# Two more ring buffers, four result tiles and back-to-back sums in a fused decoder layer

## The chip, the cores and the metric

The kernel runs on one core of a Trainium2 chip. The metric is the device time of one execution in microseconds (us), lower is better; a time is the median of several runs. On the core, TensorE (PE in the profile) multiplies matrices, and its weight loads (PEld) overlap with that; VectorE (DVE) and ScalarE (ACT) do elementwise work; GpSimd (POOL) and SyncE (SP) do little else here than issue DMAs between the chip's memory (HBM) and the on-chip SBUF. Results of the matmuls land in PSUM banks, which DVE and ACT empty. Each engine works through its own list in order; semaphores hold an instruction back until what it needs is there.

## The reference

One layer of a decoder in float32, for 1024 prompt tokens (and 16 learned meta tokens ahead of them) and 32 sample tokens: a gated short convolution and a multi-scale retention side by side, a projection, and a dense SwiGLU FFN, each behind an RMS norm. Cut to what matters:

```python
def _rmsnorm(x, g):
    y = x * lax.rsqrt(jnp.mean(x * x, axis=-1, keepdims=True) + EPS)
    return y * g

def _layer(x, ...):
    z = _rmsnorm(x, norm1_g) @ w_in                     # 1024 -> 3584
    conv_out = b_gate * conv(c_gate * h)                # 512 wide
    ret_out  = silu(g) * norm(retention(q, k, v))       # 512 wide
    x = x + concat([conv_out, ret_out]) @ w_out
    xn = _rmsnorm(x, norm2_g)
    return x + (silu(xn @ w_gate) * (xn @ w_up)) @ w_down   # 1024 -> 2816 -> 1024

y_prompt, y_sample = _rmsnorm(layer output, final_norm_g)   # and the new conv and retention states
```

## The kernel before

Activations lie transposed: 128 features on the partitions, tokens along the free axis. Every fp32 matrix product is made of three matmuls of a rounded part ("hi", tiles ending in `h` or called `whi`) and a rest ("lo", ending in `l` or called `wlo`): hi·hi, hi·lo, lo·hi. ACT makes each hi by a copy, DVE each lo by a subtraction.

The program runs in this order. First come the input projections with the two mixers, then `w_out`, which also builds the operands of the FFN. The **up phase** is a loop over 22 pairs of feature tiles (`f`, L861 on). Each takes one 2x2 step of Strassen's method in Winograd's form (`strassen`, L750): seven products instead of eight. The products go into three banks: y (`by`, four products y1 to y4), z (`bz`) and w (`bw`). Behind each product, `on` (L884) reads the bank; y3 for example is added to `up` by L894, and y4, which goes on in the same bank, cannot start before that add has read it.

What the up phase computes does not fit into SBUF. `spill` (L798) writes the operands of nine pairs of `f` to HBM (`hd`): seven operands each (b11, t3, t1, t2, t4, b21, b22), of which four are differences (`td`, L795: tiles dt3, dt1, dt2, dt4). For each operand `to_hd` (L788) takes two ring buffers, fills them (`hh` by ACT at L790, `hl` by DVE at L791), and GpSimd writes them out (L792, L793). One operand is put out at each step of the following `f`, through the generator `pending`. The last four `f` are put out plainly (`spill_plain`, tensor `hp`).

All of these are buffers of one ring: the pool `rows`, tag "u", with 60 buffers (L126, `ut`). During the up phase 56 of them hold the operands of the FFN, so that four pass the spilled pairs. A tile that takes a buffer waits until everything that used the buffer's last tile is done, the DMA that wrote it out included.

The **down phase** reads the operands back (`pull_block`, L840, `pull`, L833, tiles `hb..` and `ht..`) in four blocks into the same ring, and multiplies them by `w_down` with the same Strassen step, two output tiles (`m`, `m+1`) at a time. Its `on` adds each product to the residual `x1` (L958). SyncE issues the pulls and the loads of `w_down` (L153) in one list. A pull is issued when its buffer is free; the first block's pulls are spread over the last `f`, four at each step. The sums of weight quarters that Strassen's method needs (s1 to s4) are made by `total` at L754 on DVE.

The end is the plain part (`pd`, L999): for each of four groups of tokens (two sets of tokens, two halves) it runs through eight tiles `m`, adds to `x1` (L1004), sums the squares, and `finish` (L972) makes the final norm. `rms_compact` (L204) sums over the partitions by matmuls with a column of ones, once for each of the two partial sums (`ss3` and the last square `sq3`), and DVE combines them (L220, L222). After the root (L198 to L202) and the broadcast (`n3b`), each result tile `yt` takes two multiplies on DVE (L984), and SyncE writes it to `o_y` (L985), 256 KB. There are two `yt` buffers for four result tiles a group. The finish of the first three groups runs beside the matmuls of the next group, one step for each `m` (`tail`); that of the last has nothing beside it.

The order of the instructions on every engine is settled when the program is built, by a scheduler that knows the pools and their sizes. So a change of a pool's size moves instructions that the source leaves where they were.

Of the kernel before, what the change touches and what calls it, by code (L numbers as in the profile page):

```python
# [10 lines left out]
F32 = mybir.dt.float32  # L11
F32R = mybir.dt.float32r
AF = mybir.ActivationFunctionType
# [3 lines left out]
P = 128  # L17
# [4 lines left out]
NSAMP = NS * TS  # L22
NMETA = 16
# [6 lines left out]
HD = 64  # L30
# [10 lines left out]
SG = 544  # L41
# [5 lines left out]
HT = 528  # L47
# [71 lines left out]
def _body(nc, tc, t, offs, ncols):  # L119
    PSUM = bass.MemoryType.PSUM  # L120
    V, S, G, T, D = nc.vector, nc.scalar, nc.gpsimd, nc.tensor, nc.sync
    HW = SG // 2
    with contextlib.ExitStack() as ctx:
        cst = ctx.enter_context(tc.tile_pool(name="cst", bufs=1))
        wts = ctx.enter_context(tc.tile_pool(name="wts", bufs=4))
        rows = ctx.enter_context(tc.tile_pool(name="rows", bufs=60))  # L126
        acc = ctx.enter_context(tc.tile_pool(name="acc", bufs=3, space=PSUM))
        aux = ctx.enter_context(tc.tile_pool(name="aux", bufs=2, space=PSUM))
        dram = ctx.enter_context(tc.tile_pool(name="dram", bufs=1, space=bass.MemoryType.DRAM))
# [1 line left out]
        def ut(name, dt=F32):  # L131
            return rows.tile([P, SW], dt, tag="u", name=name)
# [71 lines left out]
        def rms_compact(sets, name):  # L204
            blocks = [(i, o, min(P, w - o)) for i, (_, w) in enumerate(sets) for o in range(0, w, P)]
            tot = len(blocks)
            ps = aux.tile([P, 512], F32, tag="aux", name=name + "p")
            a = cst.tile([P, 16], F32, tag="rms", name=name + "a", bufs=6)
            V.memset(a, 1.0)
            for q in range(len(sets[0][0])):  # L210
                for i, (c, o, n) in enumerate(blocks):
                    T.matmul(ps[:n, q * tot + i:q * tot + i + 1], sets[c][0][q][:, o:o + n], ones[:, 0:1],
                             start=True, stop=True)
                i = 0
                while i < tot:
                    j, n = i, blocks[i][2]
                    while j < tot and blocks[j][2] == n:
                        j += 1
                    if q == 0:
                        V.tensor_scalar(a[:n, i:j], ps[:n, i:j], 1.0 / DM, EPS, ALU.mult, ALU.add)  # L220
                    else:
                        V.scalar_tensor_tensor(a[:n, i:j], ps[:n, q * tot + i:q * tot + j], 1.0 / DM, a[:n, i:j],  # L222
                                               ALU.mult, ALU.add)
# [22 lines left out]
        with contextlib.ExitStack() as mid_ctx:  # L246
# [46 lines left out]
            for k in range(KT):  # L293
# [82 lines left out]
            kT = []  # L376

            vt = [mid.tile([P, 4, 512], F32, name=f"v{s}") for s in range(SETS)]
            vs = mid.tile([NSAMP, 512], F32, name="vs")
            vm = mid.tile([NMETA, 512], F32, name="vm")  # L380
            def v_rows(vT, j, s):
                pt = aux.tile([P, 4, P], F32, tag="aux", name="pvt")
                for b in range(4):
                    T.transpose(pt[:, b, :], vT[:, b * P:(b + 1) * P], ident)
                S.activation(vt[s][:, :, j * P:(j + 1) * P], pt, AF.Copy)
                if s == 0:
                    pe = aux.tile([P, 2, P], F32, tag="aux", name="pve")
                    for i, (ex, o, ne) in enumerate(((vs, 512, NSAMP), (vm, 544, NMETA))):
                        T.transpose(pe[:ne, i], vT[:, o:o + ne], ident)
                        S.activation(ex[:, j * P:(j + 1) * P], pe[:ne, i], AF.Copy)  # L390

            held = None
            for j in range(4):
# [50 lines left out]
            def meta_and_samples():  # L444
# [7 lines left out]
                ps = aux.tile([P, NPAIR, P], F32, tag="aux", name="ps0")  # L452
                kf = kmd.rearrange("p h d -> p (h d)")
                for j in range(4):
                    T.matmul(ps[:, j, :], kf[:NMETA, j * P:(j + 1) * P], vm[:, j * P:(j + 1) * P],
                             start=True, stop=True)
                for hh in range(2):
                    sl = slice(hh * HD, (hh + 1) * HD)
# [20 lines left out]
                pms = []  # L479
# [29 lines left out]
                for h in range(H):  # L509
                    for n2 in range(4):  # L510
                        T.matmul(po[:NSAMP, h, :], qx[h % 2][:, n2, h // 2, :], sst[h][:, n2 * HD:(n2 + 1) * HD],
                                 start=(n2 == 0), stop=False)
                    T.matmul(po[:NSAMP, h, :], pms[h % 2][:NSAMP, h // 2, :], vs[:, h * HD:(h + 1) * HD],
                             start=False, stop=True)
                    if h == 3:
                        yield
                yield
                d = group_norm(po, NSAMP, "sgam", "sgam2")
                for h2 in range(4):
                    pn = aux.tile([P, 2, 256], F32, tag="aux", name="psn")  # L520
                    for a in range(2):
                        h = 2 * h2 + a
                        kv = ut("kv")
                        for p in range(2):
                            G.tensor_copy(kv[:NSAMP, p * HD:(p + 1) * HD], kd[p][:NSAMP, h, :])
                        for n2 in range(4):
                            V.tensor_scalar(kv[:NSAMP, P + n2 * HD:P + (n2 + 1) * HD], vs[:, h * HD:(h + 1) * HD],
                                            tb("nsel")[:NSAMP, n2:n2 + 1], None, ALU.mult)
# [175 lines left out]

        for s in range(SETS):
            n = ntok[s]
            ss2 = late.tile([P, SG], F32, tag="rr", name="ss2", bufs=2)
            half = None
            for m in range(KT):
                x = gg("x1")  # L710
# [261 lines left out]
        def finish(s, g, ss3, q):  # L972
            n = ntok[s]
            oc = slice(OOFF[s] + g * n, OOFF[s] + (g + 1) * n)
            r, blocks = rms_compact([([ss3, q], n)], "n3")
            yield
            pb = aux.tile([P, 512], F32, tag="aux", name="n3b")
            for i, (_, o, w) in enumerate(blocks):
                T.matmul(pb[:, o:o + w], r[:w, i:i + 1].broadcast_to([w, P]), ident[:w, :w], start=True, stop=True)
            for m in range(0, KT, 2):  # L980
                yt = fin.tile([P, SG], F32, tag="yt", name="yt", bufs=2)
                y2 = yt[:, :2 * n].rearrange("p (g n) -> p g n", g=2)
                for i in range(2):
                    V.tensor_tensor(y2[:, i, :], x1[m + i][g][:, SO[s]:SO[s] + n], pb[:, :n], ALU.mult)  # L984
                D.dma_start(yo[:, m:m + 2, oc], y2)  # L985
                yield
# [91 lines left out]
```

## Time and profile before

| | |
|---|---|
| median of 3 runs | 1218.04 us (1217.74 to 1219.55) |
| the profiled execution's own time | 1217.98 us |
| its span, first to last instruction | 1216.2 us |
| mean granted TensorE clock | 0.993 |
| PE busy | 1190.3 us, 98% of the span |
| DVE, ACT, POOL busy | 844.7, 487.2, 121.3 us |
| moved by DMA | 162.91 MB, 134 GB/s on average |

The span is that of the one execution the profiler recorded; its own time has 1.8 us around the span. In the rows below, a timeline row has the start and the duration in us, engine, line, operation, and output<-inputs; "[idle before <-releaser]" is how long the engine stood still before it and what it waited for last. A row of the waits has the total, the number of times, and the longest. A row of the windows has the window, its length, each engine's busy time with the number of instructions, the granted clock (PEclk), the busy share of the DMA engines, and the GB/s moved.

### The profile page before, as it was taken

To read this page: it belongs to the slowest core of one execution; us is meant where nothing else is said; L and a number is where in the kernel's file an instruction comes from. 1 tells how busy PE (TensorE), PEld (TensorE's weight loads), DVE (VectorE), ACT (ScalarE), POOL (GpSimd) and SP (SyncE) were. 2 spreads that over 40 slices of the span, in tenths; PEclk is the share of its full clock that TensorE was granted. 3 is DMA by queue.
4 is the path that set the end of the run, shared out by engine and by line. 5 is a ranking of instruction groups with operands and counts; after the bars stand their busy time and mean duration, and the time that the engine had idled before them with its cause. 6 is when DMAs were issued, how large, how long until landed. Compare 5 with 4: busy or idle time off the path is not lost.

```text
span 1216.2 us, 22825 instructions
## 1 busy us (share of the span) xinstructions
PE 1190.3 (98%) x8903; PEld 1135.4 (93%) x8903; DVE 844.7 (69%) x1591; ACT 487.2 (40%) x932; POOL 121.3 (10%) x251
## 2 busy tenths in 40 slices
PE   8999999999999999999999999999999899999996
PEld 6998988999989998899999999999999899999996
DVE  5454467676554577877877787787876588887655
ACT  8246531121233456544443544444344222222353
POOL 0100112000100012102211221121121000000000
PEclk9999999999999999999999999999999999999998
DMA  6231211000111356425433543454254998864213
GB/s 232 80 98 35 79 36 61 27 27 27 48 46 44 99 176 195 148 71 186 151 111 137 186 151 104 145 179 144 90 191 129 388 349 271 307 212 162 93 39 106
DMA packets 82059, 162.91 MB, mean 134 GB/s; under 512 B 10702, under 2 KB 23776, under 8 KB 81952
## 3 DMA queue, kind: packets, MB, share of 16 engines
q1 hardware_dynamic: 67568, 114.57, 28.7%
q0 software_dynamic: 14384, 46.88, 11.1%
q8 instruction: 70, 1.15, 0.4%
q14 instruction: 37, 0.30, 0.1%
HBM read 113.15 MB, written 48.26 MB: 133 GB/s over the span
## 4 chain that ended last, share of the span: by engine, by line
PE 64%; issue 22%; DMA 5%; POOL 4%; DVE 3%; ACT 2%; SPq 0%; POOLq 0%; DVEq 0%; ACTq 0%
PE dy L766 8%; PE po L186 8%; PE by L766 4%; PE dz L766 4%; PE pc L186 4%; PE pd L999 4%; PE pg L186 4%; PE pq L186 4%; PE ph L186 4%; PE pv L186 4%; PE pb L186 3%; PE pk L186 3%; PE dw L766 2%; PE bz L766 2%; POOL hd L793 2%
## 5 line engine op out<-in xcount | busy, mean ns | idle before, releaser
L158 ACT ACTIVATE whi<-wraw 128x512 fp32r<-128x512 f32 (+2 forms) x198 | 115.7, 584 | 291.0 <-issue 49.8
L160 DVE TENSOR_TENSOR wlo<-wraw,whi 128x512 fp32r<-128x512 f32 (+2 forms) x198 | 124.4, 629 | 54.9 <-ACT whi L158 54.8
L158 ACT ACTIVATE whi<-s 128x512 fp32r<-128x512 f32 (+2 forms) x152 | 83.8, 552 | 162.4 <-PE by L766 47.7
L766 PE MATMUL by<-b,whi 128*128 128x256 f32 (+1 forms) x704 | 129.9, 285 | 1.4 <-DVE up L894 1.4
L766 PE MATMUL bz<-t,whi 128*128 128x256 f32 (+1 forms) x704 | 130.5, 284 | 0.3 <-DVE t L691 0.3
L766 PE MATMUL by<-t,whi 128*128 128x256 f32 (+1 forms) x704 | 130.3, 284 | 0.0
L160 DVE TENSOR_TENSOR wlo<-s,whi 128x512 fp32r<-128x512 f32 (+2 forms) x152 | 89.3, 587 | 31.6 <-ACT whi L158 31.5
L766 PEld LDWEIGHTS by<-b,whi 128*128 128x128 f32 x704 | 109.2, 188 | 2.2 <-DVE up L894 2.0
L766 PEld LDWEIGHTS bz<-t,whi 128*128 128x128 f32 x704 | 109.3, 188 | 0.5 <-DVE t L691 0.5
L766 PEld LDWEIGHTS by<-t,whi 128*128 128x128 f32 x704 | 108.9, 188 | 0.1
L766 PE MATMUL bz<-t,wlo 128*128 128x256 f32 (+1 forms) x352 | 100.1, 284 | 0.0
L766 PE MATMUL by<-b,wlo 128*128 128x256 f32 (+1 forms) x352 | 100.0, 284 | 0.0
L766 PE MATMUL by<-t,wlo 128*128 128x256 f32 (+1 forms) x352 | 100.0, 284 | 0.0
L766 PEld LDWEIGHTS by<-b,wlo 128*128 128x128 f32 x352 | 66.3, 188 | 0.0
L766 PEld LDWEIGHTS by<-t,wlo 128*128 128x128 f32 x352 | 66.3, 188 | 0.0
L766 PEld LDWEIGHTS bz<-t,wlo 128*128 128x128 f32 x352 | 66.3, 188 | 0.0
L766 PE MATMUL bw<-b,whi 128*128 128x272 f32 (+1 forms) x352 | 65.1, 284 | 0.0
L958 DVE TENSOR_TENSOR x<-x,dy 128x528 f32<-128x528 f32 x64 | 45.0, 704 | 26.0 <-PE dy L766 25.4
L792 POOL DMA_DIRECT2D hd<-hh x63 | 34.0, 540 | 271.7 <-ACT hh L790 271.3
L766 PE MATMUL dz<-ht,whi 128*128 128x256 f32 (+1 forms) x288 | 54.9, 287 | 3.9 <-ACT whi L158 3.9
L766 PE MATMUL dy<-hb,whi 128*128 128x256 f32 (+1 forms) x288 | 53.3, 284 | 2.8 <-ACT whi L158 2.8
L766 PE MATMUL dy<-ht,whi 128*128 128x256 f32 (+1 forms) x288 | 54.5, 286 | 0.1
(303 smaller groups left out, 3094.8 us busy)
## 6 DMA issues: line engine op xcount, KB each, us to landing
ht<-hd SPq DMA_DIRECT2D x72, 264.0 KB, 5.4
hd<-hh POOLq DMA_DIRECT2D x63, 264.0 KB, 3.0
hd<-hl POOLq DMA_DIRECT2D x63, 264.0 KB, 3.2
hb<-hd SPq DMA_DIRECT2D x54, 264.0 KB, 5.4
wraw<-w_in SPq DMA_DIRECT2D x54, 256.0 KB, 2.6
wraw<-w_gate SPq DMA_DIRECT2D x44, 256.0 KB, 2.6
wraw<-w_up SPq DMA_DIRECT2D x44, 256.0 KB, 2.7
wraw<-w_out SPq DMA_DIRECT2D x32, 256.0 KB, 2.8
```

The source lines that it names most:

```text
L158: S.activation(hi[:, :n], raw[:, :n], AF.Copy)
L160: V.tensor_tensor(lo[:, :n], raw[:, :n], hi.bitcast(F32)[:, :n], ALU.subtract)
L186: T.matmul(ps[:, g, :n], wt[:, sl], xk[part][:, g * n:(g + 1) * n], start=(first and i == 0), stop=(last and i == 2))
L766: T.matmul(out, wt[:, sl], rhs(s, k, key, part), start=(first and k == 0 and i == 0), stop=(k == kt - 1 and i == 2), skip_group_check=not ...
L792: G.dma_start(dst[0], hi.bitcast(F32)[:, :HT])
L793: G.dma_start(dst[1], lo.bitcast(F32)[:, :HT])
L958: V.tensor_tensor(x, x, ps, ALU.subtract if i else ALU.add)
L999: T.matmul(ps[:, 0, :n], wt[:, sl], hs[k][g][part][:, SO[s]:SO[s] + n], start=(k == 0 and i == 0), stop=(k == NPL - 1 and i == 2))
```

## The change

Five edits:

1. The ring `rows` has 62 buffers instead of 60.
2. `vs` and `vm`, two small tiles of the value projection that had room of their own in the pool `mid`, are now ring tiles (a part of a 128-row buffer is used).
3. The spill's differences (`td`) share the buffers of the tag "rr" with `ss2`, instead of having three of their own; "rr" has three buffers instead of two. By then `ss2` is done with.
4. The result tile `yt` has four buffers instead of two.
5. In `rms_compact` the ones-matmuls of all partial sums stand ahead of all DVE instructions that combine them. For a norm with one partial sum nothing changes; the final norm, `n3`, has two.

```diff
-        rows = ctx.enter_context(tc.tile_pool(name="rows", bufs=60))
+        rows = ctx.enter_context(tc.tile_pool(name="rows", bufs=62))
...
-            for q in range(len(sets[0][0])):
+            nq = len(sets[0][0])
+            for q in range(nq):
                 for i, (c, o, n) in enumerate(blocks):
                     T.matmul(ps[:n, q * tot + i:q * tot + i + 1], sets[c][0][q][:, o:o + n], ones[:, 0:1],
                              start=True, stop=True)
+            for q in range(nq):
                 i = 0
                 while i < tot:
...
-            vs = mid.tile([NSAMP, 512], F32, name="vs")
-            vm = mid.tile([NMETA, 512], F32, name="vm")
+            vs = ut("vs")
+            vm = ut("vm")
...
-            ss2 = late.tile([P, SG], F32, tag="rr", name="ss2", bufs=2)
+            ss2 = late.tile([P, SG], F32, tag="rr", name="ss2", bufs=3)
...
         def td(name):
-            return late.tile([P, HT], F32, tag="td", name=name, bufs=3)
+            return late.tile([P, SG], F32, tag="rr", name=name, bufs=3)[:, :HT]
...
-                yt = fin.tile([P, SG], F32, tag="yt", name="yt", bufs=2)
+                yt = fin.tile([P, SG], F32, tag="yt", name="yt", bufs=4)
```

The number of instructions of the layer stays; three places show how their order and their waits move. Lines from L211 on are two higher in the changed kernel.

DVE's list in the up phase, `f` = 16, between the spill's difference dt4 and the add of y3 (`up_9254<-by`). `hl_9442` belongs to dt4, `hl_9479` to b21, `hl_9514` to b22. Before:

```order
L160 TENSOR_TENSOR wlo_9451<-wraw_9247,whi_9449 128x512 [waits PE_49,Activation_49]
L791 TENSOR_TENSOR hl_9405<-dt2_9402,hh_9404 128x528 [waits DMASW3_49,DMASW0_49,DMASW4_49,DVE_49,Activation_49]
L160 TENSOR_TENSOR wlo_9486<-s4_9447,whi_9484 128x512 [waits PE_49,Activation_49]
L754 TENSOR_TENSOR s4_9692<-s2_9603,wraw_9532 128x512 [waits DMAHW0_49,DVE_49]
L791 TENSOR_TENSOR hl_9442<-dt4_9439,hh_9441 128x528 [waits DMASW5_49,Activation_49]
L791 TENSOR_TENSOR hl_9479<-up_9020,hh_9478 128x528 [waits DMASW7_49,Activation_49]
L892 TENSOR_TENSOR gt_9251<-bw_9257,gt_9251 128x528 [waits PE_49]
L160 TENSOR_TENSOR wlo_9543<-wraw_9526,whi_9541 128x512 [waits Activation_49]
L908 TENSOR_TENSOR gt_9251<-gt_9251,rstd2_3941 128x528 [waits DVE_49]
L791 TENSOR_TENSOR hl_9514<-up_9021,hh_9513 128x528 [waits DMASW2_49,DMASW6_49,DMASW1_49,Activation_49]
L894 TENSOR_TENSOR up_9254<-by_9255,up_9254 128x528 [waits PE_49]
```

The same place after the change:

```order
L160 TENSOR_TENSOR wlo_9451<-wraw_9247,whi_9449 128x512 [waits PE_49,Activation_49]
L793 TENSOR_TENSOR hl_9405<-dt2_9402,hh_9404 128x528 [waits DMASW1_49,Activation_49]
L793 TENSOR_TENSOR hl_9442<-dt4_9439,hh_9441 128x528 [waits DMASW3_49,DMASW4_49,DMASW2_49,DMASW6_49,DMASW0_49,Activation_49]
L160 TENSOR_TENSOR wlo_9486<-s4_9447,whi_9484 128x512 [waits PE_49,Activation_49]
L756 TENSOR_TENSOR s4_9692<-s2_9603,wraw_9532 128x512 [waits DMAHW0_49,DVE_49]
L793 TENSOR_TENSOR hl_9479<-up_9020,hh_9478 128x528 [waits DMASW5_49,Activation_49]
L793 TENSOR_TENSOR hl_9514<-up_9021,hh_9513 128x528 [waits DMASW7_49,Activation_49]
L894 TENSOR_TENSOR gt_9251<-bw_9257,gt_9251 128x528 [waits PE_49]
L160 TENSOR_TENSOR wlo_9543<-wraw_9526,whi_9541 128x512 [waits Activation_49]
L910 TENSOR_TENSOR gt_9251<-gt_9251,rstd2_3941 128x528 [waits DVE_49]
L896 TENSOR_TENSOR up_9254<-by_9255,up_9254 128x528 [waits PE_49]
```

`hl` of b22 no longer stands directly ahead of the add of y3 but four places earlier, ahead of the add of the w bank; `hl` of dt4 stands two places earlier, ahead of the split of s4. On ACT `hh` of dt4 likewise moves ahead of the split of s4 and the copy of y2. On GpSimd the writes of `hh` and `hl` alternate now. The waits on DMAs (DMASW) name other writes.

SP's list at the change from up to down phase: the last pulls of block 0 (`hb22`), loads of `w_down` (`wraw_10863` is the fourth for the first pair of output tiles, `wraw_11009` to `wraw_11013` the first three for the second pair), and the pulls of block 1 (`hb11`, `ht3`). Before:

```order
L835 DMA hb22_10832<-hd_3939 128x528
L153 DMA wraw_10863<-w_down 128x256
L835 DMA hb11_10885<-hd_3939 128x528
L835 DMA hb11_10906<-hd_3939 128x528
L835 DMA hb11_10929<-hd_3939 128x528
L835 DMA hb11_10948<-hd_3939 128x528
L835 DMA ht3_10967<-hd_3939 128x528
L835 DMA ht3_10988<-hd_3939 128x528
L835 DMA ht3_11007<-hd_3939 128x528
L153 DMA wraw_11009<-w_down 128x256
L153 DMA wraw_11011<-w_down 128x256
L153 DMA wraw_11013<-w_down 128x256
```

After:

```order
L837 DMA hb22_10832<-hd_3939 128x528
L153 DMA wraw_11009<-w_down 128x256
L837 DMA hb11_10885<-hd_3939 128x528
L837 DMA hb11_10906<-hd_3939 128x528
L837 DMA hb11_10929<-hd_3939 128x528
L837 DMA hb11_10948<-hd_3939 128x528
L837 DMA ht3_10967<-hd_3939 128x528
L837 DMA ht3_10988<-hd_3939 128x528
L837 DMA ht3_11007<-hd_3939 128x528
L153 DMA wraw_11011<-w_down 128x256
L153 DMA wraw_11013<-w_down 128x256
```

`wraw_11009` has moved ahead of seven pulls, while `wraw_11011` and `wraw_11013` stay at the same number of DMAs from the list's start; `wraw_10863` has moved 24 places forward, to just behind the fourth pull of block 0.

DVE's list at the very end, the last group's norm and its result tiles (`n3p` are the sums in PSUM, `n3a` the mean square, `n3r` the inverse root). Before:

```order
L220 TENSOR_SCALAR n3a_14217<-n3p_14216 128x2 [waits PE_49]
L222 SCALAR_TENSOR_TENSOR n3a_14217<-n3p_14216,n3a_14217 128x2 [waits DVE_49,PE_49]
...
L984 TENSOR_TENSOR yt_14235<-x1_10546,n3b_14232 128x256 [waits DMAHW1_49,PE_49]
L984 TENSOR_TENSOR yt_14235<-x1_10550,n3b_14232 128x256
L984 TENSOR_TENSOR yt_14239<-x1_2_1_11019,n3b_14232 128x256 [waits DMAHW2_49]
L984 TENSOR_TENSOR yt_14239<-x1_3_1_11023,n3b_14232 128x256
L984 TENSOR_TENSOR yt_14243<-x1_4_1_11179,n3b_14232 128x256 [waits DMAHW3_49,DVE_49]
L984 TENSOR_TENSOR yt_14243<-x1_5_1_11183,n3b_14232 128x256
```

After:

```order
L222 TENSOR_SCALAR n3a_14217<-n3p_14216 128x2 [waits PE_49]
L224 SCALAR_TENSOR_TENSOR n3a_14217<-n3p_14216,n3a_14217 128x2 [waits DVE_49]
...
L986 TENSOR_TENSOR yt_14235<-x1_10546,n3b_14232 128x256 [waits DMAHW7_49,PE_49]
L986 TENSOR_TENSOR yt_14235<-x1_10550,n3b_14232 128x256
L986 TENSOR_TENSOR yt_14239<-x1_2_1_11019,n3b_14232 128x256 [waits DMAHW0_49]
L986 TENSOR_TENSOR yt_14239<-x1_3_1_11023,n3b_14232 128x256
L986 TENSOR_TENSOR yt_14243<-x1_4_1_11179,n3b_14232 128x256 [waits DMAHW1_49]
L986 TENSOR_TENSOR yt_14243<-x1_5_1_11183,n3b_14232 128x256
```

The second combining instruction no longer waits for PE on its own, and the third result tile waits for the write of a tile of the group before instead of one of its own group.

More of the change, by code (lines that the diff above doesn't have):

```diff
@@ L389, in v_rows @@
                         T.transpose(pe[:ne, i], vT[:, o:o + ne], ident)
-                        S.activation(ex[:, j * P:(j + 1) * P], pe[:ne, i], AF.Copy)
+                        S.activation(ex[:ne, j * P:(j + 1) * P], pe[:ne, i], AF.Copy)
             held = None
@@ L454, in meta_and_samples @@
                 for j in range(4):
-                    T.matmul(ps[:, j, :], kf[:NMETA, j * P:(j + 1) * P], vm[:, j * P:(j + 1) * P],
+                    T.matmul(ps[:, j, :], kf[:NMETA, j * P:(j + 1) * P], vm[:NMETA, j * P:(j + 1) * P],
                              start=True, stop=True)
@@ L512, in meta_and_samples @@
                                  start=(n2 == 0), stop=False)
-                    T.matmul(po[:NSAMP, h, :], pms[h % 2][:NSAMP, h // 2, :], vs[:, h * HD:(h + 1) * HD],
+                    T.matmul(po[:NSAMP, h, :], pms[h % 2][:NSAMP, h // 2, :], vs[:NSAMP, h * HD:(h + 1) * HD],
                              start=False, stop=True)
@@ L526, in meta_and_samples @@
                         for n2 in range(4):
-                            V.tensor_scalar(kv[:NSAMP, P + n2 * HD:P + (n2 + 1) * HD], vs[:, h * HD:(h + 1) * HD],
+                            V.tensor_scalar(kv[:NSAMP, P + n2 * HD:P + (n2 + 1) * HD], vs[:NSAMP, h * HD:(h + 1) * HD],
                                             tb("nsel")[:NSAMP, n2:n2 + 1], None, ALU.mult)
```

## The prediction

> **What bounds the kernel now.** I read the page first, then PE's waits, then the windows around the longest waits, and last the timelines of the engines that PE waited for there.
>
> ```profile
> PE 1190.3 (98%) x8903; PEld 1135.4 (93%) x8903; DVE 844.7 (69%) x1591; ACT 487.2 (40%) x932; POOL 121.3 (10%) x251
> PE pk L186 <- ACT xnh L304: 4.8, 2, 4.2
> PE dz L766 <- ACT whi L158: 3.9, 1, 3.9
> PE dy L766 <- ACT whi L158: 2.8, 1, 2.8
> PE by L766 <- DVE up L894: 1.4, 1, 1.4
> PE n3b L979 <- DVE n3r L202: 1.4, 1, 1.4
> PE n3p L212 <- DVE ss L1011: 0.9, 1, 0.9
> ```
>
> PE is busy in 1190.3 of 1216.2 us, and the change leaves its matmuls as they are. So the time can only come from the 25.9 us in which PE is idle, and what lies around the span (1217.98 - 1216.2 = 1.8 us) stays. Those 25.9 us are the waits above, waits of 0.3 us and less, and the end, behind PE's last matmul. The change touches neither the 4.8 us at the start (loads and the first split) nor the length of the chain of root and broadcast (n3r). What it can touch: the 1.4 us in the up phase, the 3.9 and the 2.8 us where the up phase turns into the down phase, and the end. These are four places with different limits, so I take each by itself.
>
> **Part 1, the stall in the up phase.** It happens once, at `f` = 16:
>
> ```profile
> 841.58 0.63 ACT L158 ACTIVATE whi<-s 128x512 fp32r<-128x512 f32 x1 [0.73 <-PE by L766]
> 842.12 0.59 ACT L890 ACTIVATE up<-by 128x528 f32<-128x528 f32 x1
> 844.40 0.42 PE L766 MATMUL by<-t,whi 128*128 128x272 f32 x2
> 845.45 0.65 ACT L790 ACTIVATE hh<-up 128x528 fp32r<-128x528 f32 x1 [2.21 <-DMA hd<-hh]
> 846.81 0.65 ACT L790 ACTIVATE hh<-up 128x528 fp32r<-128x528 f32 x1 [0.20 <-DMA hd<-hh]
> 850.46 0.71 DVE L791 TENSOR_TENSOR hl<-up,hh 128x528 fp32r<-128x528 f32 x1 [1.77 <-ACT whi L158]
> 851.09 0.70 DVE L894 TENSOR_TENSOR up<-by,up 128x528 f32<-128x528 f32 x1
> 851.85 0.52 PE L766 MATMUL by<-b,whi 128*128 128x272 f32 x2 [1.44 <-DVE up L894]
> ```
>
> Product y3 starts at 844.40; y4, two products later, needs the add of y3 (L894). On DVE that add stands right behind `hl` of b22, and this one waited 1.77 us. The hi it subtracts was done at 847.46 (846.81 + 0.65), so what it waited for is its ring buffer, which by the order recycles the one from which `hh` of b21 is written out. That `hh` was itself late (2.21 us) for a buffer. With four free buffers an operand waits for the writes of the one or two before it, with six for those of two or three before. And `hl` of b22 now stands ahead of the add of the w bank, with three instructions of DVE (about 0.7 us each) between it and the add of y3.
>
> The sum: the add of y3 has to end 1.44 us earlier for the stall to go. `hl` of b22 now depends on the write of `hl` of t2, three operands before it. If DVE then runs on without the 1.77 us, the add starts at 851.09 - 1.77 = 849.3 at the latest, which is more than the 1.44 that is needed. **-1.44 us**, with -1.0 and -1.44 as bounds. The other eight spills show no wait of PE, so nothing is gained there. What is late next is product z2's end, at which y4 starts anyway; that is PE's own pace. The differences in "rr" cost nothing: three buffers as before, and `ss2` is finished with. The two small V tiles take two of the two added buffers early on, so there the ring is as it was; the reordered transposes of `vm` stand beside matmuls on PE, whose waits there are 0.3 us or less.
>
> **Part 2, from the up to the down phase.** The stretch in order:
>
> ```profile
> 950.00:958.00 8.00, 8.00 (x68) 8.00 (x67) 4.25 (x6) 0.83 (x2) 0.00 (x0) 1.00 1.05 395
> 958.00:962.00 4.00, 0.47 (x5) 0.26 (x3) 3.33 (x6) 1.72 (x4) 1.84 (x4) 1.00 1.05 378
> 962.00:966.00 4.00, 3.65 (x16) 3.49 (x17) 1.96 (x5) 1.75 (x5) 0.30 (x1) 0.61 1.05 409
> 958.46 0.71 DVE L911 SCALAR_TENSOR_TENSOR up<-up,gt 128x528 f32<-128x528 f32 x1 [0.71 <-ACT gt L909]
> 959.70 1.32 DVE L791 TENSOR_TENSOR hl<-up,hh 128x528 fp32r<-128x528 f32 x2
> 961.05 0.76 DVE L754 TENSOR_TENSOR s<-wraw 128x256 f32<-128x256 f32 x2
> 962.33 0.42 DVE L160 TENSOR_TENSOR wlo<-s,whi 128x256 fp32r<-128x256 f32 x1 [0.52 <-ACT whi L158]
> ```
>
> The first gap (3.9 us) is DVE's chain behind the last up product: the last gate, two `hl`, the sums of s, the split. Its order is the same after the change, and it waits for no ring buffer. It stays: 0. PE's half clock behind it (0.61 in 962 to 966) is covered by the second gap.
>
> ```profile
> 964.84 4.60 SPq L153 DMA_DIRECT2D wraw<-w_down  x4
> DMA to landing us min/median/max: 4.0/5.8/7.3
> 972.22 0.42 ACT L158 ACTIVATE whi<-wraw 128x256 fp32r<-128x256 f32 x1 [4.55 <-DMA wraw<-w_down]
> 972.67 0.43 DVE L160 TENSOR_TENSOR wlo<-wraw,whi 128x256 fp32r<-128x256 f32 x1 [3.19 <-ACT whi L158]
> 973.01 0.75 DVE L754 TENSOR_TENSOR s<-wraw 128x256 f32<-128x256 f32 x2
> 973.68 0.70 DVE L958 TENSOR_TENSOR x<-x,dy 128x528 f32<-128x528 f32 x1
> 974.48 0.49 PE L766 MATMUL dy<-hb,whi 128*128 128x272 f32 x2 [2.84 <-ACT whi L158]
> ```
>
> The second gap is put down to `whi`, which had long been there; what came last is the residual add (L958, ends 974.38) that reads the y bank. It stands on DVE behind a split and two sums of the next pair's weights, and these wait for `w_down`: ACT stood 4.55 us for the load. The load waits in a full queue: the DMA share is 1.05 from 950 to 966, at about 400 GB/s, so everything lands in the order in which it was asked for, one 264 KB pull in 264 x 1024 / 400e3 = 0.68 us. An earlier landing needs an earlier start of the whole stream or a place further ahead in it. Both change:
>
> The pulls of block 0 wait for ring buffers that the last products free, one buffer a k-step of three matmuls. From y3's start to where y4 could have started lie two products of eight k-steps each: (851.85 - 1.44 - 844.40) / 16 = 0.376 us a k-step. Two more buffers make each early pull wait for a buffer freed two k-steps before: 0.7 us earlier. The whole stream moves by that. And `wraw_11009` passes seven pulls (7 x 0.68 = 4.8 us), so its split is done before the gap; DVE then has only the two sums left behind the landing of the other loads, and saves the split's 0.34 us (972.67 to 973.01). Together 0.7 + 0.4 = **-1.1 us**. Bounds: 0, if the stream starts no earlier, and -2.84, if the loads come before PE needs them. I take 1.1 as nearer to what the rows of the queue give. The moved `wraw_10863` takes its 128 KB ahead of 24 pulls: 0.33 us for these, but not for the loads behind them, which have the same bytes ahead as before. The seven pulls of block 1 come 0.33 us later by `wraw_11009`; they are first used many us later.
>
> **Part 3, the end.**
>
> ```profile
> 1204.60 0.58 PE L212 MATMUL n3p<-ones,ss 128*128 128x1 f32 x4 [0.94 <-DVE ss L1011]
> 1205.52 0.58 PE L212 MATMUL n3p<-ones,sq 128*128 128x1 f32 x4 [0.34 <-DVE n3a L220]
> 1206.13 0.16 DVE L222 SCALAR_TENSOR_TENSOR n3a<-n3p,n3a 128x2 f32<-128x2 f32 x1 [0.76 <-PE n3p L212]
> 1208.18 1.42 DVE L984 TENSOR_TENSOR yt<-x,n3b 128x256 f32<-128x256 f32 x4 [0.87 <-PE n3b L979]
> 1211.24 1.46 DVE L984 TENSOR_TENSOR yt<-x,n3b 128x256 f32<-128x256 f32 x4 [1.65 <-DMA o_y<-yt]
> DMA to landing us min/median/max: 2.2/2.2/2.3
> o_y<-yt SPq DMA_DIRECT2D x4, 256.0 KB, 2.2
> GB/s 0 0 0 0 0 0 0 0 0 0 0 0 0 0 0 0 263 328 352 352 341 113 0 0 0 0 191 345 324 352 352 185 0 0 0 0 0 0 27 0
> ```
>
> Sums: the four matmuls with `sq` start 0.92 us behind those with `ss` (0.58 of work, 0.34 of waiting for L220). Back to back the 0.34 goes, but L220 then stands ahead of L222 where both are ready: L222 moves from 1206.13 to about 1205.86, **-0.27 us**. In the three earlier groups the same matmuls lie among PE's own work and gain nothing that PE waits for.
>
> Result tiles: with four buffers the eight multiplies follow each other at 0.34 us. From 1208.18 - 0.27 = 1207.91 the last ends at 1207.91 + 7 x 0.34 + 0.42 = 1210.7, where it ended at 1212.70 before: -2.0 us. But the four writes now come together. In the last row above (1205 to 1217 us in 40 slices) a pair moves at 352 GB/s, 256 KB in 0.75 us, while tiles are ready every 0.68 us. From the first slice (1209.8, now 1209.53) four take 4 x 0.75 = 2.98 us, to 1212.5; before they ended at 1214.4. That is -1.85 us with the 0.27 in it; without the limit of the bandwidth it is -2.0. I take **-1.85**, bounds -1.6 (four writes slow each other by another 0.25) and -2.0.
>
> [...]
>
> **The sum.** -1.44 - 1.1 - 1.85 = -4.4 us against the profiled 1217.98: **1213.6 us**. The median of the three runs, 1218.04, is 0.06 from that.
>
> **The rivals.**
>
> (a) *The ring gives nothing, only the end gains.* The 1.44 us is one event in nine spills, and might have been a matter of DMA timing that comes back elsewhere; the second gap might start as late as before if the last pulls wait for the last product anyway. Then 1217.98 - 1.85 = 1216.1 us, within 0.2%. For it: the queue is full from 950 on, so what gains at its head may be lost in it. Against it: the order of `hl` on DVE changes for certain. With the up stall alone gone: 1214.7.
>
> (b) *The second gap goes altogether.* If the stream starts some 2 us earlier, PE finds the add done: 1217.98 - 1.44 - 2.84 - 1.85 = 1211.8 us. The half clock between the gaps then counts. The windows have 0.50 for about 3.4 us there (0.61 in four), so PE's work in it is some 1.7 us longer, and part of the 2.84 would stay.
>
> [...]
>
> (c) *Slower: ACT is held in the spill.* `hh` of dt4 now stands ahead of the split of s4 and of L890, which copies y2 out of the y bank, and it waits for the write of `hh` of t3 to leave its buffer.
>
> ```profile
> 836.84 1.17 ACT L790 ACTIVATE hh<-dt 128x528 fp32r<-128x528 f32 x2
> DMA to landing us min/median/max: 2.3/3.0/5.9
> ```
>
> PE needs L890 done at 844.40, where y3 starts in that bank; it ended at 842.71, so 1.7 us are spare. `hh` of dt4 (0.65 us) fits into the 0.73 us in which ACT was idle, if the write, issued at 837.5 at the earliest (836.84 + 0.65), has landed by 840.85; it delays PE if it lands after 842.5, 5.0 us after that. These writes land after 3.0 us in the median, and 5.9 at the longest. At the longest, PE loses 5.9 - 5.0 = 0.9 us in each of nine spills: 1213.6 + 8.1 = 1221.7 us. It turns slower than before from 0.5 us in each (4.4 / 9). Against it: the median is 2.0 us below that point, and more free buffers spread the writes.
>
> (d) *The change does not do what it says*: the pool might be laid out so that the added buffers stay unused; the order shows `hl` of b22 moved and other waits, so I give it no chance of its own beside (a).
>
> **How the numbers follow.** The forecast 0.58; (b) in full or in part 0.15; up stall and end without the second gap (1214.7) 0.08; (a) 0.13; (c) 0.06. The bound of faster and slower, 0.2%, is about what a measurement of this kernel can tell from no change; it is 2.4 us, so faster lies below 1215.6. Faster: 0.58 + 0.15 + 0.08 = 0.81, less 0.02 for a part 3 at its worst end = 0.79; same 0.13 + 0.02 = 0.15; slower 0.06. The range goes from 1211.4 ((b) with the best end) to 1216.3 ((a) and the 0.2 us by which single runs differ); it leaves out (c).
>
> **What would show it.** In the changed profile: no wait of PE for L896 in the up phase, and on ACT no `hh` that waits 2 us for `hd`; dz with its 3.9 us as before; dy's wait at 1.7 us instead of 2.84, with `whi<-wraw` of `wraw_11009` well before it and DMA still at 1.0; one run of eight `yt` with no wait for `o_y`, the last write landing about 2 us sooner against the last matmul; no 0.34 us ahead of `sq`. The prediction is wrong if PE waits at y3 for L892 (that is (c)), if the gap of 2.84 us is unchanged (then the stream's start was not set by the ring), or if new waits of PE for `pd` appear, since `yt` comes in longer runs ahead of the adds L1004.

## The result, and the profile after

The changed kernel takes 1211.59 us (median of 7 runs, 1209.64 to 1214.83), the kernel before beside it 1217.88 us (7 runs, 1216.2 to 1221.43). The ratio is 0.9947 (95% interval 0.9933 to 0.996), 6.3 us less. The forecast was 1213.6 us, 4.4 less, in a range from 1211.4 to 1216.3: the direction and the range held, and the gain was larger than forecast.

The profiled execution of after took 1209.64 us with a span of 1207.9. PE's busy row and its longest waits:

```profile
PE 1186.2 (98%) x8903; PEld 1133.1 (94%) x8903; DVE 844.8 (70%) x1591; ACT 487.2 (40%) x932; POOL 121.4 (10%) x251
PE pk L186 <- ACT xnh L306: 4.7, 2, 4.3
PE dz L768 <- ACT whi L158: 3.6, 1, 3.6
PE dy L768 <- ACT whi L158: 2.0, 1, 2.0
PE n3b L981 <- DVE n3r L202: 1.6, 1, 1.6
PE dy L768 <- DVE x L960: 0.3, 1, 0.3
PE n3p L213 <- ACT sq L1011: 0.3, 1, 0.3
```

The wait of 1.4 us for the add of y3 is gone, and so is that of 0.9 us for the last `ss`; dz and dy are still there, dy shorter. The span fell by 8.3 us, more than the waits did: PE itself is busy 4.1 us less with the same 8903 matmuls. Most of this is the clock: the trace of before has three half-clock windows of 3.41 us ahead of the last matmuls (at 48.13, 191.49 and 962.90 us), that of after has one (at 956.51), and by an estimate from half the clock for 3.41 us each costs PE some 1.7 us. The windows of the two executions near 48 and 192 us, with columns window, length, PE busy, clock, DMA share and GB/s; before, then after:

```profile
48.00:50.00 2.00, 2.00 (x11) 0.53 0.35 97
192.00:194.00 2.00, 2.00 (x9) 0.50 0.33 118
```

```profile
48.00:50.00 2.00, 2.00 (x18) 1.00 0.44 131
192.00:194.00 2.00, 2.00 (x16) 1.00 0.19 70
```

The first profile of before had half clock at two places where the first of after had none. Two single executions are therefore no measure of the change; below, each part is read from several.

In the up phase, the place that was quoted of before (`f` = 16) now reads so, on ACT, DVE and PE:

```profile
835.78 1.25 ACT L792 ACTIVATE hh<-dt 128x528 fp32r<-128x528 f32 x2
838.17 0.59 ACT L892 ACTIVATE up<-by 128x528 f32<-128x528 f32 x1
840.43 0.65 ACT L792 ACTIVATE hh<-up 128x528 fp32r<-128x528 f32 x1 [1.14 <-DMA hd<-hh]
841.72 0.71 DVE L793 TENSOR_TENSOR hl<-up,hh 128x528 fp32r<-128x528 f32 x1 [1.39 <-DMA hd<-hl]
842.35 0.70 DVE L894 TENSOR_TENSOR gt<-bw,gt 128x528 f32<-128x528 f32 x1
844.18 0.70 DVE L896 TENSOR_TENSOR up<-by,up 128x528 f32<-128x528 f32 x1
846.31 0.41 PE L768 MATMUL by<-b,whi 128*128 128x272 f32 x2
```

`hl` of b22 still waits 1.39 us for a buffer, but it stands ahead of L894 now, and three instructions later the add of y3 is done 1.4 us before PE needs it. `hh` of dt4 (the second of the two at 835.78) runs without a wait, and L892 behind it ends at 838.76, in time for y3, whose first matmul starts at 840.47.

The second gap and the end, on SP, DVE and PE:

```profile
958.72 2.73 SPq L153 DMA_DIRECT2D wraw<-w_down  x3
966.12 0.88 DVE L756 TENSOR_TENSOR s<-wraw 128x256 f32<-128x256 f32 x2 [2.27 <-DMA wraw<-w_down]
966.91 0.70 DVE L960 TENSOR_TENSOR x<-x,dy 128x528 f32<-128x528 f32 x1
967.71 0.49 PE L768 MATMUL dy<-hb,whi 128*128 128x272 f32 x2 [2.01 <-ACT whi L158]
1197.43 0.42 DVE L1006 TENSOR_TENSOR x<-pd,x 128x256 f32<-128x256 f32 x1
1197.48 0.58 PE L213 MATMUL n3p<-ones,ss 128*128 128x1 f32 x4
1198.35 0.61 PE L213 MATMUL n3p<-ones,sq 128*128 128x1 f32 x4 [0.29 <-ACT sq L1011]
1198.99 0.16 DVE L222 TENSOR_SCALAR n3a<-n3p 128x2 f32<-128x2 f32 x1 [1.14 <-PE n3p L213]
1199.19 0.16 DVE L224 SCALAR_TENSOR_TENSOR n3a<-n3p,n3a 128x2 f32<-128x2 f32 x1
1201.24 2.74 DVE L986 TENSOR_TENSOR yt<-x,n3b 128x256 f32<-128x256 f32 x8 [0.87 <-PE n3b L981]
```

The sums still wait for `w_down`, now without a split ahead of them. (The row of dy is put down to `whi`; as in the profile of before, what came last is the residual add, which ends at 967.61.) At the end eight multiplies run in one go. Two things there were not forecast: the matmuls with `ss` start right behind the last `pd` matmul instead of 0.94 us later, and L222 starts only when all eight sums are done.

### The profile page after: what moved, and what is told of

The parts are those of the page before. It is cut to its first block, busy times and chain, and to the rows that moved or that the text cites. A ratio compares the mean times of both kernels' runs of the same rounds, so it can differ in the third digit from the quotient of the medians.

```text
span 1207.9 us, 22799 instructions
## 1 busy us (share of the span) xinstructions
PE 1186.2 (98%) x8903; PEld 1133.1 (94%) x8903; DVE 844.8 (70%) x1591; ACT 487.2 (40%) x932; POOL 121.4 (10%) x251
## 4 chain that ended last, share of the span: by engine, by line
PE 84%; issue 7%; DMA 3%; DVE 3%; POOL 1%; ACT 1%; SPq 0%; DVEq 0%; POOLq 0%; ACTq 0%
PE by L768 17%; PE bz L768 8%; PE dy L768 8%; PE po L186 6%; PE bw L768 4%; PE pk L186 4%; PE pc L186 4%; PE pd L1001 4%; PE dz L768 4%; PE pg L186 4%; PE pq L186 4%; PE pv L186 4%; PE ph L186 4%; PE pb L186 3%; PE dw L768 2%
```

## The experiments

The first runs weigh three theories. Theory A: each part is worth what its place shows over several profiles, and half clock comes by chance. Theory B: the ring moves early work, and this keeps PE at full clock. Theory C: only the end gains.

**e1_ring: the ring edits alone.**

```diff
-        rows = ctx.enter_context(tc.tile_pool(name="rows", bufs=60))
+        rows = ctx.enter_context(tc.tile_pool(name="rows", bufs=62))
...
+            vs = ut("vs")
+            vm = ut("vm")
...
+            return late.tile([P, SG], F32, tag="rr", name=name, bufs=3)[:, :HT]
```

> Only the ring edits (62 buffers, vs and vm in the ring, td with ss2); yt and the sums as before. Theory A (the ring is worth what the traces of before and after show at its places: 1.44 at y4, about 0.3 and 0.8 in the two gaps of the transition, less 0.5 of new waits in the down phase): 2.0 to 2.6 us below before, no wait of PE for L896 in the up phase, second gap about 2.0 us, two new waits of PE of 0.17 and 0.34 us near the middle of the down phase, and the wait of 1.65 us for o_y back at the end. Theory B (the ring is worth more, since the moved early work also keeps PE from its half-clock windows near 48 and 192 us): 5 us below before, with no half-clock window before 900 us. Theory C (only the end gains): within 0.5 us of before.

Measured: 1213.07 us beside 1217.55; 0.9967 (0.9954 to 0.9979), 4.0 us less. PE waits nowhere for L894, the second gap is 2.2 us. There is half clock at 189 us, so theory B falls; the interval (2.6 to 5.6 us) does not reach C's 0.5 us, which falls too. The median lies above A's 2.0 to 2.6 us, and the interval just touches them. The later wait of PE in the middle of the down phase was 1.0 us where A had 0.34.

**e2_yt4: four result tiles alone.**

```diff
-                yt = fin.tile([P, SG], F32, tag="yt", name="yt", bufs=2)
+                yt = fin.tile([P, SG], F32, tag="yt", name="yt", bufs=4)
```

> Only four result tiles. Theory A: the eight multiplies run in one go and the four writes share the bandwidth, so the time from the first multiply to the last landing falls from 6.76 us to about 5.2 us: 1.5 us below before, nothing else moves. Rival (longer runs of multiplies hold up the adds that free pd at the three earlier group ends): PE waits at pd and the gain is under 1 us.

Measured: 1213.05; 0.9971 (0.9957 to 0.9985), 3.5 us less, and no wait for `pd`. The rival falls. A was too low as well (the interval is 1.8 to 5.2 us), and something else did move. The end of this profile, on DVE and PE:

```profile
1199.59 0.96 DVE L1011 TENSOR_TENSOR ss<-ss,sq 128x256 f32<-128x256 f32 x2
1200.62 0.42 DVE L1004 TENSOR_TENSOR x<-pd,x 128x256 f32<-128x256 f32 x1
1200.69 0.58 PE L212 MATMUL n3p<-ones,ss 128*128 128x1 f32 x4
1201.31 0.16 DVE L220 TENSOR_SCALAR n3a<-n3p 128x2 f32<-128x2 f32 x1 [0.26 <-PE n3p L212]
1202.23 0.16 DVE L222 SCALAR_TENSOR_TENSOR n3a<-n3p,n3a 128x2 f32<-128x2 f32 x1 [0.76 <-PE n3p L212]
1204.28 2.74 DVE L984 TENSOR_TENSOR yt<-x,n3b 128x256 f32<-128x256 f32 x8 [0.87 <-PE n3b L979]
```

With four tiles the scheduler puts the last add to `ss` ahead of the last add to `x`, where it stood behind it before. This alone lets the `ss` matmuls start 0.8 us earlier. It is an effect of the pool's size on DVE's order, and not of the back-to-back sums.

**e3_sums: the back-to-back sums alone.**

```diff
             for q in range(nq):
                 for i, (c, o, n) in enumerate(blocks):
                     T.matmul(...)
+            for q in range(nq):
                 i = 0
```

> Only the back-to-back sums. By the prediction's own term: 0.27 us below before (from the last pd matmul to the first yt multiply 4.25 instead of 4.52 us). By the trace of after (3.85 us there): 0.67 us, if the earlier start of the ss matmuls comes from this edit, because DVE no longer puts the last x add ahead of the last ss add.

Measured: 1216.04 beside 1217.55; 0.9987 (0.9975 to 1.0), which is not told from no change. The end was 12.8 us long, within the 12.5 to 13.0 of the kernels without the edit. The rows show why:

```profile
1202.85 0.58 PE L213 MATMUL n3p<-ones,ss 128*128 128x1 f32 x4 [0.94 <-DVE ss L1013]
1204.11 0.16 DVE L224 SCALAR_TENSOR_TENSOR n3a<-n3p,n3a 128x2 f32<-128x2 f32 x1
1205.43 1.19 PE L981 MATMUL n3b<-ident,n3r 128*128 128x128 f32 x4 [1.56 <-DVE n3r L202]
```

The `ss` matmuls still started 0.94 us behind the last `pd`: the second reading, that this edit moved them, falls. From their start to the second combining instruction it is 1.26 us, where before has 1.53 (1204.60 to 1206.13): the forecast 0.27 us is there. But in this execution the broadcast ran at half clock, 1.19 us where before has 0.68. In the profile of e4_again, the kernel without the edit, the broadcast ran at half clock as well, and there the end was 13.0 us long, 0.28 more than here.

**e4_again: the kernel before.**

> The kernel before, unchanged, for the spread. If half-clock windows fall by chance (theory A), the runs spread over some 4 us with the granted clock between 0.991 and 0.996, and the windows of half clock in its profile differ in number and place from those of the first profile (48 and 192 us). If they belong to the kernel (theory B), they are at 48 and 192 us again.

Measured: 1216.26 beside 1217.55; 0.9991 (0.9979 to 1.0004). So two medians of one kernel can lie 1.3 us apart. Half clock was at 47 us and for two windows from 958 us, none at 192: its place changes from one execution to the next. The wait at y4 was different too:

```profile
PE dy L766 <- ACT whi L158: 1.7, 1, 1.7
PE by L766 <- DVE up L894: 0.5, 2, 0.3
```

Instead of one wait of 1.44 us there are three, of 0.33, 0.20 and 0.14 us, and only the last is at `f` = 16. Which spill stalls, and by how much, changes with the execution; that this follows the landing of its writes is argued, not shown.

**e5_after: the changed kernel again.**

> The changed kernel once more, for the spread and as the measure of the three kernels beside it. Theory A (in three of four profiles with 60 buffers the up phase's waits were under 1.44 us, so that part 1 was read from an unlucky execution, while the end, 2.4 us, and the transition, about 1.3 us, are lasting): 4.5 to 6 us below before; no wait of PE over 0.3 us in the up phase; first gap 3.6 us; dy after the second gap 16.3 to 16.5 us behind the first dy of the down phase (17.3 to 18.0 with 60 buffers); from the last pd matmul to the end of the span 10.2 to 10.5 us. Theory B (the first profile of after was the lucky one): stalls at y4 come back and the second gap ends as late as with 60 buffers.

Measured: 1211.28 beside 1216.91; 0.9948 (0.9928 to 0.9968). No wait in the up phase, first gap 3.6 us, end 10.5 us, as theory A had it; the second gap ended 16.6 us behind the first `dy`, 0.1 above its range. Theory B falls. With these, every part can be read from four profiles of either kind, the first two from the starts of matmuls, the end from the last `pd` matmul's end:

| us | 60 buffers (before, e4, e3, e2) | 62 buffers (after, e1, e5, e11) |
|---|---|---|
| up phase, first `by` to first `dy` | 452.9, 451.9, 452.3, 451.2 | 451.0, 450.7, 450.8, 450.7 |
| from there to `dy` behind the second gap | 17.6, 17.3, 17.7, 18.0 | 16.3, 16.5, 16.6, 16.3 |

| us | two `yt` (before, e4, e3, e1) | four `yt` (e2, e11, after, e5) |
|---|---|---|
| last `pd` matmul to the end of the span | 12.5, 13.0, 12.8, 12.8 | 10.2, 10.3, 10.5, 10.5 |

The means differ by -1.3, -1.2 and -2.4 us, -4.9 in all. Each row separates the two kinds without overlap, the first by only 0.2 us. What is not in the rows hardly differs: from the second gap to the last `pd` matmul it is 230.1 us in the mean with 60 buffers and 230.0 with 62, and ahead of the up phase 502.0 and 502.4, half clock included.

**e6_pair: `w_down` ahead of the pulls.** One DMA for two quarters, and each pair of output tiles one step ahead:

```diff
-                a11, a21 = (load_w(t["w_down"][m + i][:, at:at + w], w) for i in range(2))
-                a22, a12 = (load_w(t["w_down"][m + i][:, at + w:at + 2 * w], w) for i in (1, 0))
+                r0, r1 = (load_w(t["w_down"][m + i][:, at:at + 2 * w], 2 * w) for i in range(2))
+                return r0[:, :w], r1[:, :w], r1[:, w:2 * w], r0[:, w:2 * w]
...
+                    early_w = quarters(m + 2) if m + 2 < KT else None
```

> The changed kernel with w_down of the first three blocks loaded in rows of 256 KB (two quarters in one buffer) and each pair of output tiles loaded one step ahead, so that the second pair's weights stand ahead of the pulls in SP's list. Theory A (the second gap is the landing of w_down in a full queue): the second gap goes, 2.0 us less than after in the profile, and the waits of 0.17 to 1.0 us in the middle of the down phase go too. Rival (the queue is the bound, and what is asked for earlier only pushes the pulls back): PE waits as long for pulls (ht, hb) instead, within 0.5 us of after.

Measured: 1208.73; 0.9939 (0.9916 to 0.9962), 2.6 us below e5_after in the medians. From the down phase on, PE's only waits of over 0.3 us:

```profile
PE dz L768 <- ACT whi L158: 3.6, 1, 3.6
PE n3b L994 <- DVE n3r L202: 1.6, 1, 1.6
```

The last load for the second pair now lands 11.1 us ahead of the down phase, where in after it lands 15.4 us into it, and the second gap is gone at the same DMA share (1.04 to 1.06). So part 2's mechanism is shown: the landing of `w_down` set its end. That the queue is full was by itself no bound. The fewer, larger loads and their earlier place come together in this edit and were not tried apart.

**e7_both: the sums of the first pair ahead of the spills too.**

```diff
+                if f == NFF - 1 and step == "z2":
+                    b11, b21, b22, b12 = first
+                    for nm, p, q in (("s3", b11, b21), ("s1", b21, b22), ("s2", "s1", b11), ("s4", "s2", b12)):
+                        if nm in ("s3", "s2"):
+                            both = ut(nm)
...
```

> As e6_pair, and the sums s1 to s4 of the first pair of output tiles are made in ring buffers during the last up product instead of behind the last two spills. Theory A (the first gap is DVE's list only): the first gap of 3.6 us goes as well; with no idle stretch left there, no half-clock window at 950 to 975 us either (1.7 us each): 3.6 + 1.7 + 2.0 = 7.3 us below after. Rival (the pulls of block 0 land too late for a PE without gaps: the last of them landed 5.9 us into the down phase): PE waits for hb of b22, and 3 to 4 us of it come back, so 3 to 4 us below after.

Measured: 1210.96; 0.995 (0.9934 to 0.9966), no better than after. The first gap is gone, but:

```profile
969.49 0.70 DVE L985 TENSOR_TENSOR x<-x,dy 128x528 f32<-128x528 f32 x1 [3.12 <-DMA x<-x1d]
PE dy L770 <- DVE x L985: 3.3, 1, 3.3
```

Both theories named the wrong next bound. PE did not wait for a pull; it arrived 3.6 us sooner at the second pair, whose first residual add waited for `x1`, loaded behind seven pulls. The first gap had hidden that.

**e8_ring58: two pairs of ring buffers fewer than after.**

```diff
-        rows = ctx.enter_context(tc.tile_pool(name="rows", bufs=62))
+        rows = ctx.enter_context(tc.tile_pool(name="rows", bufs=58))
```

> The changed kernel with 58 ring buffers, which leaves one pair for the spills instead of three. Theory A (what an operand of the spill waits for is the write of the operand as many pairs before, about 3 to 4 us each, and with 60 buffers that just fits between two steps of 2.9 us): PE stalls in all nine spills, by 1 to 4 us each, so 10 to 35 us slower than after; the second gap ends about 1.4 us later than with 62. Rival (the number of buffers hardly matters, the order on DVE does): within 3 us of after.

Measured: 1223.35; 1.005 (1.0028 to 1.0072), 12 us slower than e5_after. What ACT waited for `hh`, summed over the up phase, in e8, and then in before and in after:

```profile
ACT hh L792 <- DMA hd<-hh: 74.5, 49, 6.0
```

```profile
ACT hh L790 <- DMA hd<-hh: 21.1, 22, 2.2
```

```profile
ACT hh L792 <- DMA hd<-hh: 12.9, 10, 2.0
```

With 58, 60 and 62 buffers it is 74.5, 21.1 and 12.9 us. PE stalled only once, though, not nine times as theory A had it:

```profile
695.82 0.64 ACT L792 ACTIVATE hh<-up 128x528 fp32r<-128x528 f32 x1 [5.99 <-DMA hd<-hh]
697.42 0.59 ACT L888 ACTIVATE gt<-by 128x528 f32<-128x528 f32 x1
698.06 0.39 PE L768 MATMUL by<-t,whi 128*128 128x272 f32 x1 [3.57 <-ACT gt L888]
```

`hh` held up ACT for 5.99 us, and the copy of y1 behind it came too late for PE. This is rival (c)'s chain, at y1 instead of y2, with one pair of buffers where the change has three. Half clock followed (699 us). The up phase was 456.6 us, 5.8 more than with 62, and the second gap ended 17.9 us into the down phase, 1.5 more. From the first `dy` to the last `pd` matmul it was 250.3 us, against 246.0 in after and 246.2 in e5_after, so that some 10 of the 12 us lie in these two phases. The order on DVE changes with 58 buffers too, so this run does not weigh the number of buffers alone.

**e9_all: the residual tiles one step ahead as well.**

```diff
-                if bi == 0 and m > 0:
-                    for i in range(2):
+                if bi == 0 and m + 2 < KT:
+                    for i in range(2, 4):
```

> As e7_both, and the residual tiles x1 of each pair of output tiles are loaded one step ahead, before the pulls of the next block. Theory A (what kept e7_both from its gain was the add of the second pair's first product, which waited 3.1 us for x1 behind seven pulls): that wait goes, PE has no gap over 0.5 us between 950 and 1000 us, and the kernel is 2.5 to 3.5 us below e6_pair. Rival (the queue is full, so the bytes moved ahead make the pulls of block 0 or 1 late): PE waits for ht or hb there by about as much, and the time is within 1 us of e6_pair.

Measured: 1203.79 us beside 1216.60; 0.9899 (0.988 to 0.9918). Its windows:

```profile
950.00:958.00 8.00, 8.00 (x69) 8.00 (x68) 7.86 (x17) 3.70 (x8) 1.32 (x3) 1.00 1.05 385
958.00:962.00 4.00, 4.00 (x35) 4.00 (x34) 3.90 (x9) 0.84 (x2) 0.85 (x2) 1.00 1.04 401
962.00:966.00 4.00, 3.48 (x29) 3.31 (x28) 2.79 (x7) 1.56 (x4) 0.00 (x0) 1.00 1.05 397
```

PE has a gap of 0.5 us left here (and one of 0.9 at 995 us), the clock is 1.00 in these windows, and the DMA queue is as full as ever. It is 4.6 us below e10_pair in the medians (it was expected to be 2.5 to 3.5); from the first `dy` to the last `pd` matmul it is 3.2 us, 239.5 against 242.7. It has the lowest time of all the kernels measured here.

**e10_pair: e6_pair again, beside e9_all.**

> The kernel of e6_pair once more, beside e9_all: the first gap of 3.6 us, no second gap, no wait over 0.3 us in the rest of the down phase; 6 to 9 us below before.

Measured: 1208.37 beside 1216.60; 0.9939 (0.9921 to 0.9957), 8.2 us below the median before; its waits as expected.

**e11_nosums: the change without the back-to-back sums.**

> The changed kernel with the sums interleaved as before: ring and four result tiles alone. Theory A (with four result tiles DVE's last ss add comes ahead of the last x add, so PE waits for the last square and not for L220): the end from the last pd matmul is 10.2 to 10.6 us, as in after, and the back-to-back sums are worth under 0.1 us there. By the prediction's term: 0.27 us more than after.

Measured: 1212.01; 0.9962 (0.9947 to 0.9977). The end was 10.3 us, against 10.5 with the edit. DVE's rows there:

```profile
1203.00 0.16 DVE L220 TENSOR_SCALAR n3a<-n3p 128x2 f32<-128x2 f32 x1 [0.27 <-PE n3p L212]
1203.92 0.16 DVE L222 SCALAR_TENSOR_TENSOR n3a<-n3p,n3a 128x2 f32<-128x2 f32 x1 [0.76 <-PE n3p L212]
```

Interleaved, L220 is done while PE waits for the last square. Back to back, both combining instructions come behind the eighth matmul (1198.99 and 1199.19 in after). So beside four result tiles the edit costs about 0.15 us: the first `yt` multiply starts 3.85 us behind the last `pd` matmul with it, 3.70 without. Theory A's reason was right (PE waits for the square), and its sign for the sums was not.

## Why the prediction was right, and where it was off

**Part 1** gave -1.44 from a stall of one execution. The mechanism is right: with `hl` of b22 further ahead of the add of y3, and with more buffers, there is no wait over 0.12 us in the up phase in any of the eight profiles with 62 buffers. Which of the two does it is open, since every change of the ring moved the order as well. The size was right by luck. With 60 buffers `f` = 16 stalled in all four profiles, but by 0.14 to 1.44 us, and other spills stalled too; the longest single wait ranged from 0.3 to 1.44 us. The waits come to 0.9 us in the mean, and the whole up phase became 1.3 us shorter.

**Part 2** gave -1.1, measured -1.2. e6_pair shows the cause, and the four profiles of either kind bear out both terms: the first pull of block 0 is issued 19.9 us ahead of the first `dy` instead of 19.1, and the third load for the second pair lands 15.2 us behind it in the mean instead of 16.0, about 0.85 us earlier where the working had 0.7. The remaining 0.4 us is the split that no longer stands between that landing and the residual add. That the first gap would stay was right to 0.3 us: it is 3.9 us in all four profiles with 60 buffers and 3.6 with 62. The difference lies between the first sum and ACT's split of it, which starts 0.4 us behind the sum with 60 buffers and 0.1 with 62; why is open, since the order on DVE and ACT there is the same. That the half clock behind it costs nothing was not tried with the second gap in place. Without the second gap, taking the first gap away (e9_all against e10_pair) shortened the down phase by 3.2 us, with 1.4 us of new waits.

**Part 3** is the term that was mis-sized: -1.85, measured -2.4. Some 0.3 us of that is chance: the broadcast ran at half clock in e3 and e4 (0.5 us each) and for a part in e1. "Result tiles" was right: from the first multiply to the last landing 6.76 us before and 5.24 after, -1.5 where the working had -1.58, and the four landings are 0.75 us apart, as worked out. "Sums" was right by itself, as e3_sums shows, and wrong beside four tiles: forecast -0.27, measured +0.15. The step that failed is that DVE's order ahead of the norm was taken as given. With four tiles the last `ss` add comes before the last `x` add, and the `ss` matmuls start 0.8 us earlier. L220 is then done while PE waits for the last square (0.34 us in e11), so there is no wait for L220 to be saved, and back to back both combining instructions wait for all eight matmuls. -1.5, -0.8 and +0.15 make -2.2, and that is how much sooner the last write lands behind the last `pd` matmul: 9.1 us instead of 11.3.

**The sum** by places is -4.9 against the -4.4 of the forecast. The measured 6.3 has an interval of 4.9 to 8.2, e5_after measured 5.6, and the profiles show no further place. What the medians show beyond 4.9 is open; two medians of one kernel lay 1.3 us apart.

**The rivals.** (a), only the end gains, is refuted by e1_ring. (b) did not come about: the second gap was 1.0 to 2.2 us. (c) has no trace in the changed kernel, but its chain is real, as e8_ring58 shows with fewer buffers.

**The signs.** Most came as named. Two did not: ACT still has an `hh` that waits 2.0 us for `hd` (it holds up nothing that PE needs), and dy's wait in after was 2.0 us, not 1.7.

## What to carry to other kernels

A stall read from one execution is a draw: profile the same kernel again before a single wait enters a sum, and compare whole phases. A pool's size moves instructions, so read the order of every engine from the last point that is unchanged, not only where the edit is. And when a queue is full, what matters is who stands first in it: a few weight loads moved ahead of bulk transfers took 2.6 us more off the changed kernel, and taking away the gap ahead of them gained nothing until the next late load (`x1`) was moved as well.

## What the runs showed of the hardware

In before, half clock came also where PE was never idle. PE is busy throughout from 46 to 48 us, with 18 one-column matmuls from 45.18 to 47.29, and half clock begins at 48.13 (the clock is 0.53 in the window from 48 to 50 us shown above):

```profile
45.18 2.11 PE L212 MATMUL n1p<-ones,ss 128*128 128x1 f32 x18
46.00:48.00 2.00, 2.00 (x18) 1.00 0.05 16
```

In after the same 18 matmuls run from 44.5 to 46.6 us, and the clock is 1.00 from 40 to 950 us. So the same matmuls were followed by half clock in one execution and not in another; why is open.

The second place in before is like it. Half clock begins at 191.49 us, and PE is busy throughout ahead of it:

```profile
188.00:190.00 2.00, 2.00 (x9) 1.00 0.00 0
190.00:192.00 2.00, 2.00 (x12) 0.87 0.50 144
```

Some of the matmuls there have 32 rows (`psn`, from 186.92 us on); whether that is the reason was not tried.

Of the gaps, the first one at the change to the down phase had half clock around its end in both traces: 3.9 us in before, with half clock from 962.90 to 966.32 us, and 3.6 us in after, with half clock from 956.51 to 959.92. The second gap had none, 2.8 us in before and 2.0 us in after: the clock is 1.00 from 966.32 to 1208.66 in before and from 959.92 to 1202.27 in after. What makes the difference was not tried.

The four half-clock windows ahead of the last matmuls lasted 3.413 us each. In before the clock falls at 48.13, 191.49, 962.90 and, behind the last matmul, at 1208.66 us: the later falls come 143.36, 914.77 and 1160.53 us behind the first, about 42, 268 and 340 times 3.413. In after it falls at 956.51 and, behind the last matmul, at 1202.27 us, 245.76 us or about 72 times 3.413 apart.

A kernel's spread goes with the clock: the seven runs of after go from 1209.64 us at a mean clock of 0.996 to 1214.83 at 0.991.
